# A decoder block on one core: two tiles of the next quarter's first MLP product are computed ahead of a quarter's first weight pair, and the pairs' accumulators are read ahead of the next weights' parts

## The chip, the core and the metric

The kernel runs on one core of a Trainium2 chip. The core has five engines with a queue each: TensorE (PE, matrix products; PEld is its weight load), VectorE (DVE), ScalarE (ACT), GpSimd (POOL) and SyncE (SP, which here only issues transfers). An engine works through its own queue in order, and waits where an operand or a buffer is not ready. The metric is the device time of one execution in microseconds (us), the median over runs.

## The reference

One decoder block for 512 tokens of width 1024. Two token mixers run side by side (a compressed, selected and windowed attention, and a latent attention), are merged by gates and added to x. Then comes the MLP, which the change is about:

```
h2 = modulate(rmsnorm(x1), shift, scale)          # 512 x 1024
u  = square(relu(h2 @ w_fc1))                     # w_fc1: 1024 x 4096
x2 = x1 + gate * (u @ w_fc2)                      # w_fc2: 4096 x 1024
out = rmsnorm(x2, g_final)
```

## The kernel before, in words

**Numbers.** Every float32 operand of a product is split in two parts, hi (rounded for the fast matmul) and lo (the rest), and a product is three matmuls: hi by hi, hi by lo, lo by hi. The hi part is a copy on ACT, the lo part a subtraction on DVE.

**MLP.** The 4096 inner columns are worked through in four quarters of 1024 (the loop over qq). A quarter has two stages.

*Units.* Eight tiles of the first product, in the order UNITS = 0, 4, 1, 5, 2, 6, 3, 7. One tile (`dense`, L197 to L199) has 8 blocks of 128 rows by three matmuls of 512 columns, 24 matmuls, into one accumulator of PSUM (tags acc, acc, m, o in turn). Its weights (`wsplit`, L183 hi and L184 lo) come as one transfer of 512 KB. After each tile `unit_parts` runs: relu on ACT out of the accumulator (L913), and then, for units 0 to 3, two squares (L922, L923), a difference (L924) and the parts uh and ul (L925 ACT, L926 DVE); for units 4 to 7 a square (L933), the parts uh and ul (L934, L935), and the sums and differences t3, t2 and t4 with units 0 to 3 (L942 to L944) and their parts (L946, L947, L949, L950). Unit 7 is the last, so its parts are the last that the pairs need. They all lie in 20 buffers of 512 columns (tag N) and 4 of 1024 (tag kk), and all of these are in use when a quarter's units are done.

*Pairs.* The second product of a quarter adds to x. Two column tiles of w_fc2 by two halves of the rows and two halves of the tokens are computed with seven products in place of eight (sums of weight blocks and of u's blocks, in the manner of Strassen and Winograd). One such pair has seven `product` calls of 12 matmuls of 256 columns (L854), 84 in all, into four accumulators: pa and pb (tag s, two buffers) and pc and pd (tag t, two buffers). A quarter has four pairs; the last quarter has two, and its last four column tiles are computed in the plain way by halves of the tokens, as the tail.

*Weights of a pair* (`pair_weights`, L815): two transfers of 512 KB on SP's queue, four sums on POOL (L825), and the parts (`split_part`, hi L812 on ACT, lo L813 on DVE): one part of 1024 columns for a11 and a12, four of 512 columns for the sums s1 to s4 (ws_hi, ws_lo), one of 512 columns for a22. The buffers decide how early they can be made: the sums' parts take 4 of 5 buffers of tag p per pair (hi and lo of s1 with s3, hi and lo of s2 with s4), so the next pair's are made as the present pair's products let go of them.

*Order within a pair* (`pair_tiles`). Two orders exist. In the usual one the products come as pa (a11), pb (s1), pc (s3), pd (s2), then pa again (a12), pb again (s4), pc again (a22). Between them the accumulators are read, because pa, pb and pc are added onto again: u is a copy of pa (L864), e is a copy of pc (L878) to which pb is added (L879), u gets pd (L881). pb's second product (s4) may only start once L879 has read pb. The first pair of each quarter is "fresh": its order is pa, pb, then a12, s3 and s4 by blocks of rows (units 4 to 6 first, unit 7's block last), then pd and a22, so that what unit 7 makes is wanted late; there e is a copy of pb (L867) to which pc is added (L873), and u gets pd (L875). The two accumulators of tag t go to the next pair as they are read: pc and pd of the next pair wait for L875 and L900. In the second pair of a quarter the scheduler has put pc ahead of pb on PE; in the third and fourth the usual order stands. At the end `sink` reads the accumulators into x: L894 out of pa, L896 on POOL, L898 out of pb, L900 out of pc. The next pair's pb is the same buffer of tag s as this pair's pb, and so waits for L898.

**What sets the order.** The program is written in a plain order, and a scheduler places each instruction in its engine's queue by priority; work under `tc.high_priority()` goes ahead of what is ready beside it. The weights' hi and lo parts (L183, L184, L812, L813) and the relu (L913) are under high priority; of the reads of accumulators only L873 is.

## Time and profile before

| | |
|---|---|
| median of three runs | 853.72 us (852.92 to 855.2) |
| the profiled execution's own time | 852.93 us |
| span from the first to the last instruction in it | 851.2 us |
| mean granted TensorE clock | 0.983 |
| busy: PE, DVE, ACT, POOL | 805.5, 611.8, 393.0, 151.2 us |
| pairs of quarter 1 (520.48 to 570.59) | 50.11 us |
| pairs of quarter 2 (614.15 to 658.89) | 44.74 us |
| pairs of quarter 3 (702.45 to 747.16) | 44.71 us |
| pairs of quarter 4 (790.72 to 816.57, two pairs) | 25.85 us |

1.73 us of the execution lie outside the span. A stage of pairs is counted from the end of the last unit's matmuls to the end of the last pair's. In a row of the timeline, the first number is the start in us from the span's start, the second the duration; in brackets stands the time for which the engine stood idle ahead of it, with what ended that. In a row of the windows view stand the window, its length, and for each engine the busy time with the number of instructions, then the granted clock, the share of busy DMA engines and the GB/s. The waits view gives the total, the times and the longest of each kind.

### The profile page before, as it was taken

What the parts mean: (1) busy time and instruction counts of PE and PEld (TensorE: products, weight loads), DVE (VectorE), ACT (ScalarE), POOL (GpSimd) and SP (SyncE); (2) the same over time, 40 slices, a digit from 0 to 9 for tenths busy, and PEclk for the clock granted to TensorE, in tenths of its full rate; (3) what the DMA queues carried; (4) which work ended last, traced back from release to release, by engine and by line L of the source; (5) the groups of instructions that cost most, each with busy time, mean ns of one, the idle gap of its engine ahead of it and who ended that gap; (6) DMA issues with size and microseconds to landing.
All of it is one profiled execution on the core that took longest, in us unless ns stands there. A gap on an engine that the chain in (4) does not pass through costs nothing.

```text
span 851.2 us, 11895 instructions
## 1 busy us (share of the span) xinstructions
PE 805.5 (95%) x4444; PEld 650.0 (76%) x4444; DVE 611.8 (72%) x1177; ACT 393.0 (46%) x742; POOL 151.2 (18%) x125
## 2 busy tenths in 40 slices
PE   6899999999999999999989998899989998999996
PEld 3687668665586657887769996898789887988895
DVE  6969569878658874568785859775777577756754
ACT  4458436555226442222323457335643565355651
POOL 2400000000001000003300023612352154414200
PEclk8999999999999999999999998999999999999998
DMA  9773342100132214587564212232223322322202
GB/s 340 254 252 112 126 148 66 34 26 26 49 126 73 74 38 161 174 273 225 174 220 172 75 50 75 98 103 97 88 74 115 122 75 75 124 100 84 90 1 99
DMA packets 31004, 99.76 MB, mean 117 GB/s; under 512 B 3521, under 2 KB 5761, under 8 KB 30946
## 3 DMA queue, kind: packets, MB, share of 16 engines
q1 hardware_dynamic: 30880, 98.89, 34.6%
q8 instruction: 35, 0.57, 0.3%
q0 software_dynamic: 64, 0.11, 0.1%
q14 instruction: 23, 0.19, 0.1%
q10 hardware_dynamic: 2, 0.00, 0.0%
HBM read 96.89 MB, written 2.10 MB: 116 GB/s over the span
## 4 chain that ended last, share of the span: by engine, by line
PE 61%; DVE 15%; DMA 7%; issue 6%; ACT 5%; POOL 5%; SPq 0%; POOLq 0%; DVEq 0%; ACTq 0%
PE ps_acc L197 8%; PE ps_acc L198 8%; PE ps_acc L199 8%; PE ps_s L854 7%; PE ps_t L854 4%; DMA w_raw<-in_w_ada_dram 4%; PE ps_t L391 3%; PE ps_o L568 3%; DVE junk L107 3%; POOL wsum L825 3%; DMA w_raw<-in_w_fc_dram 3%; PE ps_s L640 2%; DVE ws_lo L813 2%; DVE w_lo L184 2%; PE ps_o L653 2%
## 5 line engine op out<-in xcount | busy, mean ns | idle before, releaser
L183 ACT ACTIVATE w_hi<-w_raw 128x1024 fp32r<-128x1024 f32 x76 | 80.3, 1058 | 134.9 <-PE ps_acc L198 86.5
L184 DVE TENSOR_TENSOR w_lo<-w_raw,w_hi 128x1024 fp32r<-128x1024 f32 x76 | 96.5, 1271 | 60.9 <-ACT w_hi L183 60.6
L346 ACT ACTIVATE p<-p,nm 128x128 f32<-128x128 f32 (+3 forms) x96 | 53.3, 556 | 58.1 <-DVE nm L344 56.8
L198 PE MATMUL ps_acc<-hl,w_hi 128*128 128x512 f32 x200 | 80.1, 401 | 0.0
L199 PE MATMUL ps_acc<-hh,w_lo 128*128 128x512 f32 x200 | 80.0, 400 | 0.0
L197 PE MATMUL ps_acc<-hh,w_hi 128*128 128x512 f32 x200 | 79.3, 397 | 0.0
L812 ACT ACTIVATE ws_hi<-wsum 128x512 fp32r<-128x512 f32 x56 | 35.2, 631 | 65.6 <-POOL wsum L825 55.7
L379 DVE COPY pT<-ps_t 128x512 f32<-128x512 f32 (+1 forms) x72 | 42.4, 598 | 31.0 <-PE ps_o L568 16.5
L825 POOL TENSOR_TENSOR wsum<-w_raw 128x512 f32<-128x512 f32 x28 | 40.4, 1442 | 102.1 <-DMA w_raw<-in_w_fc_dram 94.1
L825 POOL TENSOR_TENSOR wsum<-wsum,w_raw 128x512 f32<-128x512 f32 x28 | 47.5, 1697 | 35.7 <-DVE ws_lo L813 35.4
L107 DVE SCALAR_TENSOR_TENSOR junk<-w_raw,cb 128x1024 bf16<-128x1024 f32 x32 | 40.0, 1255 | 18.6 <-DMA w_raw<-in_w_ada_dram 18.6
L813 DVE TENSOR_TENSOR ws_lo<-wsum,ws_hi 128x512 fp32r<-128x512 f32 x56 | 46.8, 867 | 7.2 <-PE ps_acc L198 6.3
L198 PEld LDWEIGHTS ps_acc<-hl,w_hi 128*128 128x128 f32 x200 | 37.6, 188 | 10.9 <-issue 4.3
L854 PE MATMUL ps_t<-t,ws_hi 128*128 128x256 f32 x224 | 41.2, 282 | 4.9 <-DVE ue L875 4.9
L199 PEld LDWEIGHTS ps_acc<-hh,w_lo 128*128 128x128 f32 x200 | 37.6, 188 | 10.0 <-issue 3.1
L197 PEld LDWEIGHTS ps_acc<-hh,w_hi 128*128 128x128 f32 x200 | 37.6, 188 | 9.9 <-issue 3.0
L197 PE MATMUL ps_acc<-h2h,w_hi 128*128 128x512 f32 x112 | 43.6, 390 | 0.0
L199 PE MATMUL ps_acc<-h2h,w_lo 128*128 128x512 f32 x112 | 43.6, 389 | 0.0
L198 PE MATMUL ps_acc<-h2l,w_hi 128*128 128x512 f32 x112 | 43.6, 389 | 0.0
L758 POOL TENSOR_TENSOR yb<-ya,yb 128x512 f32<-128x512 f32 x8 | 17.5, 2184 | 135.1 <-DVE yb L757 125.0
L854 PE MATMUL ps_s<-uh,w_hi 128*128 128x256 f32 x112 | 33.1, 296 | 7.9 <-ACT uh L925 6.8
L391 PEld LDWEIGHTS ps_t<-ident,p 128*128 128x128 f32 x240 | 27.7, 141 | 16.4 <-issue 6.3
(471 smaller groups left out, 2313.7 us busy)
## 6 DMA issues: line engine op xcount, KB each, us to landing
w_raw<-in_w_fc_dram SPq DMA_DIRECT2D x64, 512.0 KB, 3.3
w_raw<-in_w_ada_dram SPq DMA_DIRECT2D x32, 512.0 KB, 4.3
w_raw<-in_w_z_dram SPq DMA_DIRECT2D x25, 512.0 KB, 3.5
w_ada<-in_w_ada_dram SPq DMA_DIRECT2D x16, 512.0 KB, 6.1
w_raw<-in_w_c_dram SPq DMA_DIRECT2D x8, 512.0 KB, 4.4
w_raw<-in_w_o_dram SPq DMA_DIRECT2D x8, 512.0 KB, 4.4
w_raw<-in_w_out_dram SPq DMA_DIRECT2D x8, 512.0 KB, 3.4
w_raw<-in_w_g_dram SPq DMA_DIRECT2D x8, 448.0 KB, 6.9
```

Of the source, the lines that this page charges most:

```text
L107: nc.vector.scalar_tensor_tensor(junk, w, 1.0, cb, op0=ALU.mult, op1=ALU.mult, accum_out=mod[:, col:col + 1])
L183: nc.scalar.activation(hi[:, :n], raw[:, :n], AF.Copy)
L184: nc.vector.tensor_tensor(lo[:, :n], raw[:, :n], f(hi[:, :n]), op=ALU.subtract)
L197: nc.tensor.matmul(out, w[0], x[0], start=first, stop=False)
L198: nc.tensor.matmul(out, w[0], x[1], start=False, stop=False)
L199: nc.tensor.matmul(out, w[1], x[0], start=False, stop=last)
L346: nc.scalar.activation(o, o, AF.Exp, bias=nm, scale=-1.0, accum_out=sm)
L379: nc.vector.tensor_copy(dst, src)
L391: nc.tensor.transpose(pp[:, off:off + P], aps[i][:, kb * P:(kb + 1) * P], ident)
L813: nc.vector.tensor_tensor(lo, src, f(hi), op=ALU.subtract)
L825: nc.gpsimd.tensor_tensor(t, sums[x_] if isinstance(x_, int) else x_, y_, op=ALU.add)
L854: nc.tensor.matmul(out, w[a_][:, k], x[k][b_], start=(first and k == 0 and j == 0), stop=(k == 3 and j == 2), skip_group_check=True)
```

## The change

**Two tiles ahead of the first pair.** After a quarter's last unit, in the first three quarters, the first two tiles of the next quarter's first product (units 0 and 4) are computed and their relu is taken, before the quarter's first pair. Their relus need a place to stay (`held0`, `held1`): the first takes a buffer of tag qst; for the second, four small tiles of an earlier stage (w2, th, hd, rep) are put together into two buffers of a new tag "common", one of which is free by then. What follows the relu for these two units (the squares, parts and sums) is written at its place in the next quarter's loop; the relu is taken out of `unit_parts` into `unit_relu`.

**One order for the pairs.** The fresh order goes; every pair has the usual one.

**Reads ahead of parts.** In `pair_tiles` the copies of pa and pc, the additions of pb and pd, and the whole sink stand under high priority.

```diff
-    w2 = sb.tile([P, 2, 2, 64], F32, name="w2")
+    def common(name):
+        return sb.tile([P, S], F32, name=name, tag="common", bufs=2)
+
+    w2_th, hd_rep = common("w2_th"), common("hd_rep")
+    w2 = w2_th[:, 0:256].rearrange("p (k n c) -> p k n c", k=2, n=2)
...
-        th = sb.tile([P, 256], F32, name="th", tag="th")
+        th = w2_th[:, 256:512]
...
-    def pair_tiles(w, b, sink, fresh):
+    def pair_tiles(w, b, sink):
...
         product(pa, w["a11"], b["11"], True)
-        nc.scalar.activation(u, pa, AF.Copy)
+        with tc.high_priority():
+            nc.scalar.activation(u, pa, AF.Copy)
         product(pb, w["s1"], b["t1"], True)
-        if fresh:
-            nc.scalar.activation(e, pb, AF.Copy)
-            for ks in (range(3), range(3, 4)):
-                product(pa, w["a12"], b["21"], False, ks)
-                product(pc, w["s3"], b["t3"], True, ks)
-                product(pb, w["s4"], b["22"], False, ks)
-            with tc.high_priority():
-                nc.vector.tensor_tensor(e, e, pc, op=ALU.add)
-            product(pd, w["s2"], b["t2"], True)
-            nc.vector.tensor_tensor(u, u, pd, op=ALU.add)
-        else:
-            product(pc, w["s3"], b["t3"], True)
+        product(pc, w["s3"], b["t3"], True)
+        with tc.high_priority():
             nc.scalar.activation(e, pc, AF.Copy)
             nc.vector.tensor_tensor(e, e, pb, op=ALU.add)
-            product(pd, w["s2"], b["t2"], True)
+        product(pd, w["s2"], b["t2"], True)
+        with tc.high_priority():
             nc.vector.tensor_tensor(u, u, pd, op=ALU.add)
-            product(pa, w["a12"], b["21"], False)
-            product(pb, w["s4"], b["22"], False)
+        product(pa, w["a12"], b["21"], False)
+        product(pb, w["s4"], b["22"], False)
         product(pc, w["a22"], b["t4"], False)
-        sink(pa, pb, pc, u, e)
+        with tc.high_priority():
+            sink(pa, pb, pc, u, e)
...
-        pair_tiles(w, ub, sink, n == 0)
+        pair_tiles(w, ub, sink)
...
+    held = {}
     for qq in range(4):
...
         for i, n in enumerate(UNITS):
+            if i in held:
+                unit_parts(n, held[i], ub, keep, qq == 3)
+                continue
...
-            unit_parts(n, pa, ub, keep, qq == 3)
+            unit_parts(n, unit_relu(pa, tmp("relu")), ub, keep, qq == 3)
+
+        held = {}
+        if qq < 3:
+            for i in range(2):
+                w = wsplit(d["w_fc1"][8 * qq + 8 + UNITS[i]], (KT, P))
+                pa = psum("acc")
+                dense(pa, w, h2)
+                r = sb.tile([P, S], F32, name=f"held{i}", tag="qst", bufs=NB["qst"]) if i == 0 else common("held1")
+                held[i] = unit_relu(pa, r)
         nf = KT - NH2 if qq == 3 else KT
         for n in range(0, nf, 2):
             fc2_pair(qq, n)
```

The lines move by a few: the sums of weights L825 become L829, the parts L812 and L813 become L816 and L817, the products L854 become L858, the copies L864 and L878 become L869 and L873, the additions L879 and L881 become L874 and L877, the sink's L894, L898 and L900 become L891, L895 and L897, and the relu L913 becomes L908.

Three places show how the queues change. The first is ACT's queue at the end of the second quarter's units, before: the relu of unit 7 (`relu<-ps_o`), its square, its uh, and the parts t of t3 and t24, with the first pair's reads of pa (`ue<-ps_s`, L864 and L867) among them.

```order
L812 ACTIVATE w_hi<-w_raw 128x1024
L913 ACTIVATE relu<-ps_o 128x512
L933 ACTIVATE relu<-relu 128x512
L864 ACTIVATE ue<-ps_s 128x256
L934 ACTIVATE uh_5458<-relu 128x512
L946 ACTIVATE t_5466<-b_5119 128x256
L949 ACTIVATE t_5469<-ur_5419 128x512
L867 ACTIVATE ue<-ps_s 128x256
L812 ACTIVATE w_hi<-w_raw 128x512
```

The same place of the changed kernel; `held` is the kept relu of the next quarter's units 0 and 4.

```order
L908 ACTIVATE relu<-ps_o 128x512
L816 ACTIVATE ws_hi<-wsum 128x512
L932 ACTIVATE relu<-relu 128x512
L933 ACTIVATE uh_5453<-relu 128x512
L945 ACTIVATE t_5461<-b_5180 128x256
L948 ACTIVATE t_5464<-ur_5414 128x512
L816 ACTIVATE w_hi<-w_raw 128x512
L908 ACTIVATE held_5498<-ps_acc 128x512
L921 ACTIVATE b_6065<-held_5498 128x256
L922 ACTIVATE ur_6068<-held_5498 128x256
L816 ACTIVATE w_hi<-w_raw 128x1024
L908 ACTIVATE held_5531<-ps_acc 128x512
```

Unit 7's parts now stand ahead of every read of the first pair's accumulators, and the two held relus with the first squares of the next quarter stand between them and the first pair.

The second is DVE's queue in the first pair of the second quarter, before; xr is a tile of x, v a temporary of the sink.

```order
L894 SCALAR_TENSOR_TENSOR xr_3166<-ps_s,modb,xr_3166 128x256
L873 TENSOR_TENSOR ue<-ue,ps_t 128x256
L813 TENSOR_TENSOR ws_lo<-wsum,ws_hi 128x512 x2
L813 TENSOR_TENSOR w_lo<-w_raw,w_hi 128x512
L813 TENSOR_TENSOR ws_lo<-wsum,ws_hi 128x512 x2
L875 TENSOR_TENSOR ue<-ue,ps_t 128x256
L900 TENSOR_TENSOR v_5598<-ue,ps_t 128x256
L813 TENSOR_TENSOR w_lo<-w_raw,w_hi 128x1024
L898 TENSOR_TENSOR v_5600<-ue,ps_s 128x256
```

And of the changed kernel.

```order
L817 TENSOR_TENSOR w_lo<-w_raw,w_hi 128x1024
L817 TENSOR_TENSOR ws_lo<-wsum,ws_hi 128x512 x2
L874 TENSOR_TENSOR ue<-ue,ps_s 128x256
L877 TENSOR_TENSOR ue<-ue,ps_t 128x256
L891 SCALAR_TENSOR_TENSOR xr_3161<-ps_s,modb,xr_3161 128x256
L817 TENSOR_TENSOR w_lo<-w_raw,w_hi 128x512
L817 TENSOR_TENSOR ws_lo<-wsum,ws_hi 128x512 x2
L895 TENSOR_TENSOR v_5661<-ue,ps_s 128x256
L897 TENSOR_TENSOR v_5659<-ue,ps_t 128x256
```

The read of pd (L875), which stood behind five parts, is gone; what stands in this pair now is what stood in the other pairs before, with the next pair's parts of 1024 and of two sums ahead of the read of pb (L874) and three parts ahead of the read of pb at the end (L895).

The third is DVE's queue in the last pair of the second quarter of the changed kernel, where the held units' parts are made; the first row belongs to the next quarter's unit weights.

```order
L184 TENSOR_TENSOR w_lo<-w_raw,w_hi 128x1024
L925 TENSOR_TENSOR ul_6067<-ur_6068,uh_6066 128x512
L934 TENSOR_TENSOR ul_6075<-held_5531,uh_6074 128x512
L942 SCALAR_TENSOR_TENSOR ur_6068<-ur_6068,held_5531 128x256
L946 TENSOR_TENSOR t_6082<-b_6065,t_6082 128x256
L943 SCALAR_TENSOR_TENSOR ur_6068<-ur_6068,held_5531 128x256
L874 TENSOR_TENSOR ue<-ue,ps_s 128x256
L877 TENSOR_TENSOR ue<-ue,ps_t 128x256
```

Five operations of the held units stand ahead of the last pair's read of pb; before, only the row of L184 stood there. On PE every pair of the changed kernel has the order pa, pb, pc, pd, a12, s4, a22.

More of the change, by code (lines that the diff above doesn't have):

```diff
@@ L443, in hidden @@
             nc.tensor.transpose(pt[:, n * P:(n + 1) * P], th[:, n * P:(n + 1) * P], ident)
-        hd = sb.tile([P, 2, 2, 2, 32], F32, name="hd", tag="hd")
-        nc.vector.tensor_copy(hd.rearrange("p n k g b -> p (n k g b)"), pt[:, 0:256])
+        hd = hd_rep[:, 0:256].rearrange("p (n k g b) -> p n k g b", n=2, k=2, g=2)
+        nc.vector.tensor_copy(hd_rep[:, 0:256], pt[:, 0:256])
         pk = psum("m")
@@ L458, in hidden @@
             for n in range(2):
-                rep = sb.tile([P, 4, 32], F32, name="rep", tag="rep", bufs=2)
+                rep = hd_rep[:, 256 + 128 * n:384 + 128 * n].rearrange("p (r b) -> p r b", r=4)
                 nc.gpsimd.tensor_copy(rep, hd[:, n, 1, g, :][:, None, :].to_broadcast([P, 4, 32]))
@@ L907, in fc2_pair, with unit_relu, unit_parts @@
                 nc.scalar.activation(xt[j], xt[j], AF.Copy, scale=cols[:, C_GFIN + j:C_GFIN + j + 1])
-    def unit_parts(n, pa, ub, keep, last):
-        r = tmp("relu")
+    def unit_relu(pa, r):
         with tc.high_priority():
             nc.scalar.activation(r, pa, AF.Relu)
+        return r
+    def unit_parts(n, r, ub, keep, last):
         hh = big_n(f"uh{n}", F32R)
```

## The prediction

> **What bounds the kernel now.** The page's busy line comes first.
>
> ```profile
> span 851.2 us, 11895 instructions
> PE 805.5 (95%) x4444; PEld 650.0 (76%) x4444; DVE 611.8 (72%) x1177; ACT 393.0 (46%) x742; POOL 151.2 (18%) x125
> ```
>
> PE is the bound: 95% busy. The change adds and removes no matmul, so it can only save time in which PE stands idle or runs slowly. The page's mean does not say where that is; the windows view does. Its first four rows are the pair stages of the four quarters; the fifth is the last pair of quarter 2, in which PE waits for nothing.
>
> ```profile
> 520.48:570.59 50.11, 43.70 (x337) 42.19 (x336) 38.30 (x63) 22.40 (x41) 19.00 (x15) 0.93 0.29 95
> 614.15:658.89 44.74, 40.92 (x337) 39.91 (x336) 34.66 (x55) 19.66 (x35) 18.32 (x14) 1.00 0.28 95
> 702.45:747.16 44.71, 40.92 (x337) 39.91 (x336) 34.69 (x55) 19.63 (x35) 18.31 (x14) 1.00 0.28 95
> 790.72:816.57 25.85, 22.64 (x170) 21.63 (x169) 20.14 (x34) 15.38 (x29) 4.04 (x4) 0.93 0.17 62
> 648.95:658.89 9.94, 9.94 (x86) 9.94 (x85) 6.63 (x13) 2.89 (x4) 0.74 (x1) 1.00 0.36 121
> ```
>
> A pair without waits takes 9.94 us, so 84 matmuls at 0.118 us. Four take 39.76, two take 19.88. What the stages have above that is all the change can reach: 50.11 - 39.76 = 10.35 in quarter 1, 4.98 in quarter 2, 4.95 in quarter 3, 25.85 - 19.88 = 5.97 in quarter 4, together 26.25 us. The waits view of PE from 519 us on names what ends the idle time (total us, times, longest):
>
> ```profile
> PE ps_s L854 <- ACT uh L925: 6.8, 5, 2.7
> PE ps_t L854 <- DVE ue L875: 4.9, 4, 1.5
> PE ps_s L854 <- DVE v L898: 2.9, 7, 0.6
> PE ps_s L854 <- ACT ue L864: 1.1, 1, 1.1
> ```
>
> Four causes: a quarter's first pair finds unit 3's parts uh and ul unfinished; the second pair's pc waits until the first pair's pd is read (L875); a pair's pb waits until the last pair's is read (L898); in quarter 4 PE waits once for the copy L864. PE's timeline gives the places. In quarters 1 and 2:
>
> ```profile
> 522.13 0.39 PE L854 MATMUL ps_s<-uh,w_hi 128*128 128x256 f32 x1 [0.79 <-ACT uh L925]
> 526.10 0.58 PE L854 MATMUL ps_s<-uh,w_hi 128*128 128x256 f32 x1 [2.70 <-ACT uh L925]
> 616.46 0.38 PE L854 MATMUL ps_s<-uh,w_hi 128*128 128x256 f32 x1 [1.08 <-ACT uh L925]
> 617.19 0.39 PE L854 MATMUL ps_s<-ul,w_hi 128*128 128x256 f32 x1 [0.34 <-DVE ul L926]
> 629.13 0.51 PE L854 MATMUL ps_t<-t,ws_hi 128*128 128x256 f32 x2 [1.51 <-DVE ue L875]
> 631.36 0.38 PE L854 MATMUL ps_s<-uh,ws_hi 128*128 128x256 f32 x1 [0.58 <-DVE v L898]
> ...
> 640.42 0.38 PE L854 MATMUL ps_s<-uh,ws_hi 128*128 128x256 f32 x1 [0.31 <-DVE v L898]
> ...
> 650.38 0.28 PE L854 MATMUL ps_s<-uh,ws_hi 128*128 128x256 f32 x1
> ```
>
> A wait costs more than its idle time: matmuls start 0.118 apart, but a row lasts 0.28 (the last one), so the row ahead of a wait counts 0.16 as busy that is lost, and the first one behind it is up to 0.10 longer. I take 0.23 together, an estimate. And two entries cost clock:
>
> ```profile
> 527.00:531.00 4.00, 4.00 (x19) 4.00 (x20) 3.94 (x6) 3.22 (x7) 0.97 (x1) 0.50 0.01 4
> 793.80:797.80 4.00, 4.00 (x21) 4.00 (x22) 3.74 (x7) 3.69 (x8) 0.97 (x1) 0.58 0.03 12
> ```
>
> After 0.79 and 2.70 of idle time quarter 1's entry ran at half the clock: 19 matmuls in 4 us, where 34 fit.
>
> [...]
>
> **The change, part by part.** *Two tiles ahead of the first pair.* They are moved, not added; their 48 matmuls are the same. What they bring is cover: ACT's copies of unit weights stand one tile apart,
>
> ```profile
> 576.04 1.06 ACT L183 ACTIVATE w_hi<-w_raw 128x1024 fp32r<-128x1024 f32 x1 [4.31 <-PE ps_acc L198]
> 581.48 1.06 ACT L183 ACTIVATE w_hi<-w_raw 128x1024 fp32r<-128x1024 f32 x1 [2.02 <-PE ps_acc L198]
> ```
>
> so a tile is 5.44 us and two are 10.88. Against it stands the time that the last units' parts need after the last unit's matmuls. Unit 3's, for which pa waited, took until 526.10 - 520.48 = 5.6 us; the last of all, unit 7's, until 530.33 + 0.68 - 520.48 = 10.5 us in quarter 1, the worst:
>
> ```profile
> 530.33 0.68 DVE L950 TENSOR_TENSOR t<-ur,t 128x512 fp32r<-128x512 f32 x1
> ```
>
> That is in time for the pair's start, and unit 7's t3 and t24 are only wanted by pc and pd, 2.84 and 4.26 us later (24 and 36 matmuls). So the entries' waits and quarter 1's lost clock go. In ACT's queue the held relus and squares stand behind unit 7's parts and ahead of the reads of pa; the last of them needs matmuls that end as the pair begins, and pa must be read by the 48th matmul, 5.68 us later: hidden by those. The two transfers of 512 KB go on SP's queue ahead of the pairs' instead of behind them; the pairs' stages use 0.28 of the DMA engines, so I cost that at nothing. Without that cover it would be a transfer's landing in three places, 3.3 us each by the page's row:
>
> ```profile
> w_raw<-in_w_fc_dram SPq DMA_DIRECT2D x64, 512.0 KB, 3.3
> ```
>
> *The fresh order goes.* With it L875 goes, which came behind five parts for the next pair, the last of them slow:
>
> ```profile
> 626.36 2.38 DVE L813 TENSOR_TENSOR ws_lo<-wsum,ws_hi 128x512 fp32r<-128x512 f32 x2
> 628.67 0.41 DVE L875 TENSOR_TENSOR ue<-ue,ps_t 128x256 f32<-128x256 f32 x1
> ```
>
> The first pair becomes what the others are. What such a pair asks of DVE I read in pair 2 of quarter 2, after which PE does not wait (650.38 above):
>
> ```profile
> 644.23 1.28 DVE L813 TENSOR_TENSOR ws_lo<-wsum,ws_hi 128x512 fp32r<-128x512 f32 x2
> 645.43 0.41 DVE L879 TENSOR_TENSOR ue<-ue,ps_s 128x256 f32<-128x256 f32 x1
> 647.88 0.69 DVE L813 TENSOR_TENSOR w_lo<-w_raw,w_hi 128x512 fp32r<-128x512 f32 x1 [1.08 <-ACT w_hi L812]
> 648.49 1.29 DVE L813 TENSOR_TENSOR ws_lo<-wsum,ws_hi 128x512 fp32r<-128x512 f32 x2
> 649.69 0.41 DVE L898 TENSOR_TENSOR v<-ue,ps_s 128x256 f32<-128x256 f32 x1
> ```
>
> Let T be a pair's start without waits; its pb starts at T + 1.42, so here T = 640.42 - 1.42 = 639.00. The first two sums' parts for the next pair need a buffer that s3 lets go of after 36 matmuls, T + 4.26; here they began at T + 5.23. The read of pb (L879) ended at 645.84, T + 6.84; s4, which waits for it, comes after 60 matmuls, T + 7.10. The last read (L898) ended at 650.10, T + 11.10; the next pb wants it after 96 matmuls, T + 11.36. Both were in time by 0.26 us, in a pair that began its parts 0.97 later than the buffers allow. So a pair of this order has from 0.26 to 1.2 us to spare, and I forecast mostly no wait.
>
> *Reads ahead of parts.* The queues show that DVE still has the next pair's parts ahead of the read of pb (L874) and three ahead of the last one (L895), as in pair 2; what priority gains is that no more work slips between. The waits on L898 are 2.9 us in seven places. From both sides, what stays of them in a quarter is nothing, or 0.58 and 0.31 with 0.23 each, 1.35. I keep 0.58, nearer to pair 2's row without a wait than to the other end. In the last pair of a quarter five operations of the held units stand ahead of the read of pb: two ul at 0.69 and three at 0.42, 2.6 us. They need buffers that pb's operands let go of at T + 2.84, and an ACT copy first, of this kind:
>
> ```profile
> 795.45 0.63 ACT L934 ACTIVATE uh<-relu 128x512 fp32r<-128x512 f32 x1
> ```
>
> So 2.84 + 0.63 + 2.64 + 0.41: the read ends at T + 6.5, 0.6 before s4. The last pair makes no sums' parts that would stand there too. If that cover goes, it costs what it is late.
>
> *Quarter 4.* Nothing is held here, so its entry stays, with these rows:
>
> ```profile
> 793.07 0.39 PE L854 MATMUL ps_s<-uh,w_hi 128*128 128x256 f32 x1 [1.13 <-ACT uh L925]
> 793.80 0.39 PE L854 MATMUL ps_s<-ul,w_hi 128*128 128x256 f32 x1 [0.34 <-DVE ul L926]
> 806.08 0.50 PE L854 MATMUL ps_t<-t,ws_hi 128*128 128x256 f32 x2 [0.40 <-DVE ue L875]
> 806.94 0.39 PE L854 MATMUL ps_s<-uh,ws_hi 128*128 128x256 f32 x1 [0.24 <-DVE v L898]
> 812.20 0.39 PE L854 MATMUL ps_s<-uh,w_hi 128*128 128x256 f32 x1 [1.10 <-ACT ue L864]
> ```
>
> The three lower rows go: 0.40 + 0.24 + 1.10 and about 0.23 behind each, 2.4 us. (The last waits for a copy, which now has priority on ACT.) The two upper rows stay, 1.47 + 0.46 = 1.93, and the rest of the 5.97, 1.6, is the lost clock. New here: the usual order wants unit 7's t3 after 33 matmuls, not 51. Its lo part is this row:
>
> ```profile
> 797.27 0.41 DVE L947 TENSOR_TENSOR t<-t,t 128x256 fp32r<-128x256 f32 x1
> ```
>
> It ends at 797.68; with the clock kept PE would want it at 790.72 + 1.93 + 33 x 0.118 = 796.5, so a wait of 1.1 and 3.3 left with its 0.23. With the clock lost as now, PE comes to it 1.6 later and hardly waits: 3.5 left. Should both come, 4.9. I take 3.3.
>
> **The sum.** Quarter 1: 10.35 - 0.58 = 9.77. Quarter 2: 4.98 - 0.58 = 4.40. Quarter 3: 4.95 - 0.58 = 4.37. Quarter 4: 5.97 - 3.3 = 2.67. Together 21.2 us. The profiled execution took 852.93 with a span of 851.2; 851.2 - 21.2 = 830.0 of span, 831.7 of time. The median of the runs, 853.72, is 0.79 above the profiled one: **832.5 us**. The lower bound is all 26.25 gone: 827.5.
>
> **Rivals.** *Waits of the usual order come back (0.17).* The entries' gain stays, but s4 or the next pb waits in more pairs, since L875's 1.51 and L898's 0.58 and 0.31 had DVE's load as their cause, and that load is the same; 0.26 us is little to spare. Three waits of 2.40 together, as quarter 2 has now, with 0.23 each are 3.09 a quarter in place of 0.58: +7.5 for three quarters, 840.0. Against it: pair 2 left no wait though its parts began late.
>
> *DVE's parts are stretched (0.05).* Here are the two ends of one part's duration, alone and beside POOL's sums (ns, least, median, most):
>
> ```profile
> L813 DVE TENSOR_TENSOR ws_lo<-wsum,ws_hi x56: 677/686/1781, 497.8 to 805.0; 128x512 fp32r<-128x512 f32 x56
> ```
>
> Were both parts ahead of the read of pb stretched in each pair, it would end at 4.26 + 2 x 1.78 + 0.41 = 8.23 against 7.10: 1.13 idle and 0.23, in ten pairs (three in each of quarters 1 to 3, one in quarter 4) 13.6 us: 846.1. Against it: the median is near the least.
>
> [...]
>
> *Slower (0.04).* The next pair's parts (L817) stand ahead of the read of pb (L874) in nine pairs of quarters 1 to 3 and one of quarter 4. If they make s4 wait for about 1.5 us, PE may lose its clock there, as in quarter 4's entry after 1.47 of idle time. That entry cost 1.93 + 1.6 = 3.53; ten such places are 35.3 against the gain of 21.2: 832.5 + 35.3 = 867.8. It decides from 2.1 us a place on, so where L874 ends later than T + 8.6 and the clock goes. Against it: quarter 2 had 1.51 of idle time at L875 and kept clock 1.00.
>
> *No net change (0.04).* The held tiles' cover fails: unit 7's parts run as late as before, because the held relus and the pairs' parts go ahead of them by priority. Then the entries cost as now, and what L875 cost is won and spent again on s4: within 2.6 us of 853.7. Against it: ACT's order has unit 7's parts ahead of the held relus.
>
> **How the numbers follow.** Forecast 0.70, the rivals 0.17, 0.05, 0.04 and 0.04. Of the forecast's own range the lower end is 828 (all waits gone), the upper 837.5 (in three quarters 0.77 more, the other end for L898, and nothing won in quarter 4, 2.67); with the first rival the range is 828 to 842, and 0.8 of the chance lies in it. 0.3%, 2.6 us, is about what a measurement of this kernel can tell from no change. Faster by more: the forecast and the two first rivals, 0.92. Within: 0.04. Slower: 0.04.
>
> **What would show it.** Right: no wait of PE for uh or ul (L924, L925) in the pairs of quarters 1 to 3; clock 1.00 in quarter 1's pairs; pair stages of about 40.3 us in quarters 1 to 3, and 23.2 in quarter 4; no wait named for L874 above 0.3 us. Wrong: PE waits for L874 or for L895 in several pairs of a quarter (first or second rival, told apart by the duration of the parts ahead); a clock under 0.95 in quarters 2 or 3 (third); waits for uh at the pairs' start (fourth). A span above 842 would say that the order of the pairs costs more than I read from pair 2.

## The result, and the profile after

The changed kernel takes **831.36 us** in the median (828.15 to 832.16), the kernel before 853.44 in the same comparison (852.92 to 855.2): a ratio of 0.973, with a 95% interval from 0.970 to 0.976. The forecast was 832.5, with a range from 828 to 842. The profiled execution has a span of 829.8 us, 21.4 less than before; 830.0 was forecast.

The page of the changed kernel, its first lines:

```profile
span 829.8 us, 11895 instructions
PE 798.3 (96%) x4444; PEld 646.3 (78%) x4444; DVE 606.2 (73%) x1177; ACT 392.1 (47%) x742; POOL 148.0 (18%) x125
```

The windows view, the pair stages of the four quarters (columns as in the prediction):

```profile
530.21:572.12 41.91, 40.59 (x338) 39.77 (x336) 36.01 (x58) 20.92 (x38) 18.48 (x16) 1.00 0.35 114
615.67:655.37 39.70, 39.70 (x337) 39.69 (x336) 32.78 (x54) 19.36 (x35) 16.85 (x14) 1.00 0.33 107
698.93:738.71 39.78, 39.78 (x337) 39.78 (x336) 32.66 (x53) 19.35 (x35) 16.74 (x14) 1.00 0.33 107
771.39:794.92 23.53, 20.87 (x170) 20.07 (x169) 19.52 (x35) 16.27 (x30) 4.03 (x4) 1.00 0.22 68
```

In quarters 2 and 3 PE is busy for the whole stage: four pairs in 39.70 and 39.78 us, where four pairs without a wait were reckoned at 39.76. The clock is 1.00 in all four stages. What the stages have above 39.76 (and 19.88 for the two pairs of quarter 4) fell from 26.25 us to 2.15 - 0.06 + 0.02 + 3.65 = 5.76. That is 20.5 of the 21.4 us of span. The rest lies outside these stages: the first pair started at 530.21, of which 10.88 are the two moved tiles, so 1.15 earlier than before, and what follows the last pair took 0.25 longer. In the profiles below that start, less the tiles moved ahead of it, lies anywhere between 516.4 and 520.9, and between 516.7 and 519.3 in the change's own two profiles; so I compare stages and give the ratio of the times beside them.

The waits view of PE from 510 us on shows what is left:

```profile
PE ps_s L858 <- ACT uh L924: 1.6, 1, 1.6
...
PE ps_s L858 <- DVE v L895: 0.6, 2, 0.4
PE ps_s L858 <- ACT ue L869: 0.5, 1, 0.5
PE ps_t L858 <- DVE t L946: 0.4, 1, 0.4
PE ps_s L858 <- DVE ul L925: 0.3, 1, 0.3
PE ps_t L858 <- ACT t L945: 0.3, 1, 0.3
...
PE ps_s L858 <- DVE ue L874: 0.2, 1, 0.2
```

The waits for uh, ul and t are those of quarter 4's entry; the others lie in quarter 1. The wait on the read of pd, 4.9 us before, is gone.

### The profile page after: what moved, and what is told of

Read it like the earlier page. It is cut to its first block, busy times and chain, and to the rows that moved or that the text cites. A ratio compares the mean times of both kernels' runs of the same rounds, so it can differ in the third digit from the quotient of the medians.

```text
span 829.8 us, 11895 instructions
## 1 busy us (share of the span) xinstructions
PE 798.3 (96%) x4444; PEld 646.3 (78%) x4444; DVE 606.2 (73%) x1177; ACT 392.1 (47%) x742; POOL 148.0 (18%) x125
## 4 chain that ended last, share of the span: by engine, by line
PE 74%; DVE 11%; DMA 5%; ACT 3%; POOL 3%; issue 3%; SPq 0%; DVEq 0%; POOLq 0%; ACTq 0%
PE ps_acc L197 10%; PE ps_acc L199 10%; PE ps_acc L198 10%; PE ps_s L858 8%; PE ps_t L858 6%; PE ps_t L391 4%; DVE junk L107 3%; PE ps_o L572 3%; DMA w_raw<-in_w_ada_dram 3%; PE ps_s L644 2%; PE ps_o L657 2%; PE ps_s L197 1%; PE ps_s L198 1%; PE ps_s L199 1%; POOL yb L762 1%
## 5 line engine op out<-in xcount | busy, mean ns | idle before, releaser
L184 DVE TENSOR_TENSOR w_lo<-w_raw,w_hi 128x1024 fp32r<-128x1024 f32 x76 | 96.1, 1266 | 62.8 <-ACT w_hi L183 62.4
L816 ACT ACTIVATE ws_hi<-wsum 128x512 fp32r<-128x512 f32 x56 | 35.3, 631 | 58.0 <-POOL wsum L829 55.3
L829 POOL TENSOR_TENSOR wsum<-w_raw 128x512 f32<-128x512 f32 x28 | 39.5, 1410 | 64.9 <-DMA w_raw<-in_w_fc_dram 53.4
L829 POOL TENSOR_TENSOR wsum<-wsum,w_raw 128x512 f32<-128x512 f32 x28 | 45.9, 1640 | 25.6 <-DVE ws_lo L817 25.2
L817 DVE TENSOR_TENSOR ws_lo<-wsum,ws_hi 128x512 fp32r<-128x512 f32 x56 | 42.9, 796 | 4.9 <-ACT ws_hi L816 2.5
L858 PE MATMUL ps_t<-t,ws_hi 128*128 128x256 f32 x224 | 40.5, 281 | 0.7 <-DVE t L946 0.4
L817 DVE TENSOR_TENSOR w_lo<-w_raw,w_hi 128x1024 fp32r<-128x1024 f32 (+1 forms) x28 | 31.0, 1107 | 10.2 <-ACT w_hi L816 10.2
```

Of the source, the lines that this page charges most:

```text
L184: nc.vector.tensor_tensor(lo[:, :n], raw[:, :n], f(hi[:, :n]), op=ALU.subtract)
L817: nc.vector.tensor_tensor(lo, src, f(hi), op=ALU.subtract)
L829: nc.gpsimd.tensor_tensor(t, sums[x_] if isinstance(x_, int) else x_, y_, op=ALU.add)
L858: nc.tensor.matmul(out, w[a_][:, k], x[k][b_], start=(first and k == 0 and j == 0), stop=(k == 3 and j == 2), skip_group_check=True)
```

## The experiments

All stages in us, from the windows view of each run's profile; "above" is the sum of what the four stages have above pairs without waits.

| run | median | ratio to before (95%) | Q1 | Q2 | Q3 | Q4 | above |
|---|---|---|---|---|---|---|---|
| before | 853.44 | | 50.11 | 44.74 | 44.71 | 25.85 | 26.25 |
| the change | 831.36 | 0.973 (0.970 to 0.976) | 41.91 | 39.70 | 39.78 | 23.53 | 5.76 |
| the change again | 830.39 | 0.973 (0.971 to 0.976) | 41.58 | 39.70 | 39.78 | 23.17 | 5.07 |
| held tiles alone | 847.23 | 0.993 (0.991 to 0.995) | 49.21 | 43.68 | 43.50 | 26.41 | 23.64 |
| held tiles, squares behind | 843.60 | 0.991 (0.988 to 0.994) | 46.53 | 42.78 | 42.79 | 25.68 | 18.62 |
| held tiles, own order, priority | 846.31 | 0.993 (0.990 to 0.995) | 48.87 | 44.04 | 43.89 | 24.33 | 21.97 |
| one order with priority, nothing held | 841.31 | 0.986 (0.984 to 0.989) | 47.25 | 42.30 | 42.39 | 23.17 | 15.95 |
| the change without priority | 829.67 | 0.973 (0.971 to 0.976) | 41.25 | 39.71 | 39.80 | 23.61 | 5.21 |
| one held tile | 833.02 | 0.977 (0.974 to 0.980) | 44.83 | 39.78 | 39.70 | 23.51 | 8.66 |
| two more on DVE per pair | 847.15 | 0.995 (0.993 to 0.997) | 47.13 | 44.84 | 44.84 | 24.88 | 22.53 |
| second pair's parts and more behind | 832.26 | 0.976 (0.974 to 0.978) | 42.09 | 40.43 | 39.85 | 23.11 | 6.32 |
| the same without the third group | 833.02 | 0.978 (0.975 to 0.980) | 42.33 | 40.44 | 40.07 | 23.65 | 7.33 |
| rearranged in quarter 4 alone | 828.11 | 0.972 (0.970 to 0.974) | 41.57 | 39.79 | 39.69 | 21.60 | 3.49 |

Four more operations on DVE per pair: 878.27, 1.031 (1.026 to 1.035); there some matmuls of the next units stand between the last pair's, so its stages are not comparable.

Each stage comes from one profile. The medians fall by 0.6 to 3.2 us more than the stages do, and of all fourteen profiles the one before has the second latest start of the MLP; so of a difference between runs I take from the stages what it is made of, and its size only roughly.

### The held tiles alone

```diff
-        pair_tiles(w, ub, sink)
+        pair_tiles(w, ub, sink, n == 0)     # pair_tiles as in the kernel before
```

> The two held tiles alone; the first pair of each quarter keeps its own order and no read of an accumulator has priority beyond what it had before. My theory (the stages' excess is two separate things: the entries, 7.2 us in quarter 1 and 1.9 in each of quarters 2 and 3, and the first pairs' waits on L875 and L898, 3.1 in each): the entries' 11.0 us go, the 3.1 stay: about 842.4, with waits of PE on the addition of pd (1.5 each) still in the trace and none on uh or ul in quarters 1 to 3. Rival (the order and the priorities bring nearly all, the tiles only move the wait): 850 or more. Rival (the tiles alone do it): 833 or less.

847.23, between my 842.4 and the first rival's 850: 2.6 us less in the stages, not 11.0 (3.2 in quarters 1 to 3, and quarter 4, where nothing is held, took 0.6 more). The windows view of the first two stages and of 4 us in the first, ACT's timeline there, and PE's:

```profile
528.59:577.80 49.21, 43.07 (x337) 42.26 (x336) 36.21 (x58) 21.12 (x38) 19.38 (x16) 0.93 0.29 97
621.36:665.04 43.68, 40.72 (x337) 39.92 (x336) 33.33 (x54) 19.54 (x35) 18.12 (x14) 1.00 0.28 98
535.00:539.00 4.00, 3.99 (x18) 4.00 (x19) 0.00 (x0) 0.23 (x1) 0.54 (x1) 0.50 0.02 8
```
```profile
531.87 0.42 ACT L928 ACTIVATE b<-held 128x256 f32<-128x256 f32 x1
...
534.05 0.63 ACT L939 ACTIVATE held<-held 128x512 f32<-128x512 f32 x1
534.59 0.36 ACT L868 ACTIVATE ue<-ps_s 128x256 f32<-128x256 f32 x1
```
```profile
535.01 0.58 PE L858 MATMUL ps_s<-uh,w_hi 128*128 128x256 f32 x1 [3.41 <-ACT ue L868]
```

The waits on uh and ul are gone, and a new one has come in their place: pa's second product, which the first pair's own order wants after 24 matmuls, waits 3.41 us for the copy of pa. That copy stands on ACT behind unit 7's parts, both held relus and the held units' squares, up to 534.59. The clock falls to 0.50 behind it, as it did at the entry before. The read of pd still costs its 1.5 to 1.9 in each of quarters 1 to 3.

### The held units' squares behind the first pair's copies

```diff
+                with tc.issue_after(first.ins):      # the first pair's copy of pb
-                unit_parts(n, held[i], ub, keep, qq == 3)
+                    unit_parts(n, held[i], ub, keep, qq == 3)
```

> The held tiles with the first pair's own order, as in the run of the held tiles alone (847.23), but the held units' squares (two of 256 columns and one of 512 on ACT) are queued behind the first pair's copies of pa and pb. PE's and POOL's queues are the same. In the run of the held tiles alone pa's second product, which this order wants after 24 matmuls, waited 3.41, 0.54 and 0.45 us for the copy of pa, which stood on ACT behind unit 7's parts and these squares. My theory (the held tiles' own work on ACT took up the place of the wait they removed; the usual order hides it since it wants pa's second product only after 48 matmuls): the three squares are 0.9 to 1.3 us on ACT, so the two waits of 0.5 go and quarter 1's falls to some 2.1: 2 to 4 us less, 843 to 845. Rival (unit 7's parts alone hold the copy up): no change, 847.

843.6, and PE's timeline has:

```profile
533.26 0.38 PE L858 MATMUL ps_s<-uh,w_hi 128*128 128x256 f32 x1 [1.99 <-ACT ue L868]
```

3.41 became 1.99, the waits of 0.5 in quarters 2 and 3 went, 5.0 us in the stages (0.7 of them in quarter 4, which the edit does not touch), 3.6 in the median. So the held tiles' own work on ACT was part of the new wait; unit 7's parts, the held relus and two parts of weights still stand ahead of the copy.

### Held tiles, the first pair's own order, and priority for the reads

```diff
         if fresh:
...
-            nc.vector.tensor_tensor(u, u, pd, op=ALU.add)
+            with tc.high_priority():
+                nc.vector.tensor_tensor(u, u, pd, op=ALU.add)     # and so for the other reads
```

> Held tiles, and all reads of accumulators under high priority, but the first pair of each quarter keeps its own order. In DVE's queue the read of pd now stands ahead of the last two of the five parts that it stood behind. My theory (L875 was late for its place behind parts, not for the order itself): most of 1.7 us goes in each of quarters 1 to 3 and 0.6 in quarter 4: 836 to 838. Rival (the order itself costs the wait): as with the held tiles alone, 842.

846.31, no better than the held tiles alone, as the rival has it. In PE's timeline of quarter 2 the wait on the read of pd is gone, and these have come:

```profile
636.31 0.39 PE L858 MATMUL ps_s<-uh,ws_hi 128*128 128x256 f32 x1 [2.04 <-DVE v L909]
...
640.05 0.48 PE L858 MATMUL ps_t<-t,ws_hi 128*128 128x256 f32 x2 [0.73 <-DVE v L911]
```

L909 and L911 are the sink's reads of pb and pc. The parts that the read of pd overtook now stand in front of these. In this order pb and pc are finished late and the next pair wants their buffers early; which read stands first only chooses where PE waits.

### One order with priority, and nothing held

```diff
-        if qq < 3:
+        if False:
```

> One order for all pairs and the priorities, without the held tiles. My theory: 2.8 us a quarter are won in the pairs and 2.3 in quarter 4, but at the entries, which stay, the usual order wants unit 7's t3 earlier and waits some 1.2 us for it in each quarter: 846, with waits on uh, ul and t3 at every entry, and a lost clock in quarter 1. Rival (the order needs the tiles' cover and costs more than it brings without it): 853 or more. Rival (order and tiles add up without a new wait): 842.

841.31, better than the 846 of my theory and close to its last rival. PE's waits view has, beside 1.4 for ul, these two:

```profile
PE ps_s L858 <- ACT uh L924: 6.6, 5, 2.7
...
PE ps_t L858 <- DVE t L946: 1.2, 3, 0.4
```

Within the pairs nothing is left: not a wait on L874 or L895. 10.3 us go in the stages, of them 2.3 to 2.9 in each quarter. The new wait on t3 that I had put at 1.2 a quarter is there, but only 0.4 at a time: PE comes late to it, since uh has held it up before.

The two single parts bring 2.6 and 10.3 us in the stages, together 12.9. The change brings 20.5 to 21.2. Some 8 us are their working together. By the medians the two bring 5.8 and 11.8 and the change 22.1, so 4.5 us together, with some 2 us of uncertainty on each of the three: that the parts need each other is shown, how much it is worth is known only roughly.

### The change without the priority

```diff
-        with tc.high_priority():
-            sink(pa, pb, pc, u, e)
+        sink(pa, pb, pc, u, e)               # and so for the four reads above it
```

> The change without the priorities on the reads. The queues of PE, DVE and POOL are then the same as the change's, row for row; on ACT eleven rows stand elsewhere (a hi part ahead of the copies of pa and pc in place of behind them). My theory: nothing depends on these, 831.4 within 1.5. Rival (the reads' priority is what keeps s4 from waiting): PE waits for the addition of pb in several pairs, 836 or more.

829.67, the ratio of the change to the last digit that counts. The waits of PE in its pairs:

```profile
PE ps_s L858 <- ACT uh L920: 1.4, 1, 1.4
...
PE ps_s L858 <- DVE v L891: 0.6, 2, 0.4
...
PE ps_s L858 <- DVE ue L872: 0.2, 1, 0.2
```

The second thing that the change is named after, reads ahead of the weights' parts, moves eleven rows on ACT and none elsewhere, and does nothing that can be measured.

### One held tile

```diff
-            for i in range(2):
+            for i in range(1):
```

> The change with one held tile in place of two, so 5.44 us of cover in place of 10.88. My theory (cover has to reach to the last part of unit 7 that pc wants, not only to unit 3's parts): waits for t3 come, some 3 us in quarter 1 and 1 in each of quarters 2 and 3: 834 to 837. Rival (unit 3's parts were all that was late, 2 to 5.6 us): within 1 of the change. Rival (it is worth half): 841.

833.02, 2.9 us more than the change in the stages, all of it in quarter 1. The windows view of stages 1 and 2, and PE's timeline in stage 1:

```profile
523.20:568.03 44.83, 42.17 (x337) 41.35 (x336) 36.92 (x61) 21.64 (x39) 16.98 (x14) 0.96 0.32 106
611.59:651.37 39.78, 39.78 (x337) 39.75 (x336) 32.95 (x53) 18.18 (x33) 16.66 (x14) 1.00 0.33 107
```
```profile
526.24 0.39 PE L858 MATMUL ps_s<-uh,w_hi 128*128 128x256 f32 x1 [1.78 <-ACT uh L924]
```

One tile is enough in quarters 2 and 3. The second earns its place in quarter 1 alone, and not by t3, as I had it: unit 3's uh is late there even with 5.44 us of cover.

### Two and four more operations on DVE in each pair

```diff
             nc.scalar.activation(e, pc, AF.Copy)
+            for _ in range(2):               # 4 in the other run
+                nc.vector.tensor_tensor(e, e, e, op=ALU.max)
             nc.vector.tensor_tensor(e, e, pb, op=ALU.add)
```

The lines that hold PE's matmuls to the change's order are left out here.

> The change with two more operations on VectorE in each pair ahead of the read of pb: the larger of e and e, which leaves e as it is, 256 columns each, so 0.66 to 0.8 us later. PE's queue is held to the same order. In the trace of the change the read of pb ends 1.13, 0.75, 0.27 and 0.9 us before s4 in the four pairs of quarter 2. My theory (what counts is the time to spare at s4, and VectorE's idle time behind it makes good the rest): only the third pair waits, 0.4 with 0.2 for the refill: 1 to 3 us more in all. Rival (VectorE is the bound in the pairs, any work added to it shows): 14 pairs at 0.7, 10 us more. Rival (there is no time to spare, each pair waits): 14 pairs at 0.7 + 0.23, 13 more.

> The same with four operations, 1.33 to 1.6 us later. My theory (time to spare of 0.3 to 1.1 at s4): waits of 0.2 to 1.1 with 0.2 for the refill in nearly every pair, some 3.4 a quarter, 8 to 13 us more than the change. Rival (VectorE as the bound): 20 more. Rival (more time to spare than read): under 3 more.

847.15 and 878.27, 16 and 47 us more than the change: far above my theory's 1 to 3 and 8 to 13, and above the rivals too. First the size of the added operation with two of them (ns: least, median, most), then DVE's and POOL's timelines and PE's in the first pair of quarter 2:

```profile
L877 DVE TENSOR_TENSOR ue<-ue x28: 410/1158/1512, 537.0 to 806.8; 128x256 f32<-128x256 f32 x28
```
```profile
625.41 1.51 DVE L877 TENSOR_TENSOR ue<-ue 128x256 f32<-128x256 f32 x1
626.85 0.41 DVE L881 TENSOR_TENSOR ue<-ue,ps_t 128x256 f32<-128x256 f32 x1
627.18 1.16 DVE L877 TENSOR_TENSOR ue<-ue 128x256 f32<-128x256 f32 x1
```
```profile
624.97 1.67 POOL L829 TENSOR_TENSOR wsum<-wsum,w_raw 128x512 f32<-128x512 f32 x1 [1.06 <-DVE ws_lo L817]
626.60 1.45 POOL L829 TENSOR_TENSOR wsum<-w_raw 128x512 f32<-128x512 f32 x1
```
```profile
628.85 0.38 PE L860 MATMUL ps_s<-uh,ws_hi 128*128 128x256 f32 x1 [1.72 <-DVE ue L878]
```

The dose was larger than written: 0.41 us alone, 1.51 and 1.16 beside POOL's sums, and the scheduler put the read of pd (0.33 from its start to the next) between. So the read of pb came 1.51 + 0.33 + 1.16, about 3 us later, against the 1.13 to spare that I had read: some 1.8 should be left as a wait, and 1.72 is there. The other pairs of that quarter agree: counted from the pair's start the read ended 2.96, 2.57, 1.44 and 0.20 us later than in the change, with 1.13, 0.75, 0.27 and 0.9 to spare, and PE waited 1.72, 1.71, 0.97 and nothing. The mechanism stands, the time to spare was read rightly, and the added time was not. PE waits for nothing else in the pairs of quarters 2 and 3, so the rival that any work on DVE shows fails: of 3 us only the part above the time to spare does.

With four, the read of pb is 2.8 to 5.0 us late in ten pairs, and the clock falls. The waits view, and the windows behind two of these waits, one of 4.97 us and one of 3.50:

```profile
PE ps_s L860 <- DVE ue L878: 33.5, 10, 5.0
```
```profile
544.50:548.50 4.00, 3.66 (x18) 3.66 (x19) 1.29 (x3) 0.63 (x1) 0.81 (x2) 0.57 0.40 131
659.00:663.00 4.00, 3.73 (x32) 3.73 (x33) 2.31 (x6) 0.63 (x1) 1.91 (x2) 1.00 0.34 131
```

This is the slower rival's mechanism, brought about by force: 26 us more than before. Its condition, a wait of about 1.5 us, was put too short: with two operations, five waits of 1.7 us and one of 3.17 lost no clock; with four, eight of ten waits from 2.76 to 4.97 did, and those ending at 659 and 672 did not. The last section says what tells them apart.

### Looking for what is left: three rearrangements

The first puts the second pair's parts, the tail's four copies and the held units' parts behind chosen instructions on ACT and DVE; the second leaves out the third group. The change ran beside them once more.

```diff
+        with behind(ends):          # ends: unit 7's last parts on ACT and DVE, for the second pair
-        split_part(raw[0], hi, lo)
+            split_part(raw[0], hi, lo)
...
+        with behind(keep["end"]):
-        nc.scalar.activation(hi, b12, AF.Copy)
+            nc.scalar.activation(hi, b12, AF.Copy)
...
+                with behind(first):
-                unit_parts(n, held[i], ub, keep, qq == 3)
+                    unit_parts(n, held[i], ub, keep, qq == 3)
```

> The change itself once more, beside the two kernels after it. 0.973 of the kernel before, about 831; pair stages as in its first profile (41.9, 39.7, 39.8, 23.5 us) within 0.7, while the start of the first pair may differ by up to 3 us from 530.2, as it did among the runs so far, for reasons that lie ahead of the MLP.

> The change, with three groups of work queued behind a chosen instruction on ACT and DVE: the parts of a quarter's second pair and the four copies for the tail (L995, L996 in the change) behind unit 7's last parts, and the held units' parts behind the first pair's copy of pc and read of pb. In the change's trace quarter 4's ACT stood idle for 2.02 us in front of a hi part of the second pair, with unit 6's square and unit 3's relu queued behind it; unit 3's uh came 1.65 us late and unit 7's t3 0.67. My theory (quarter 4's 3.65 us and quarter 1's 2.15 come from this place in the queues): quarter 4's stage falls from 23.5 to 20.5 to 21.5, quarter 1's from 41.9 to 40.3 to 41.3: 2.5 to 4.5 us less than the change. Rival (the second pair's parts, made later, are late for that pair): waits on them or on the reads of pb there, no gain. Rival (the entry of quarter 4 is bound by unit 3's own chain of five operations): under 1 us less.

> The same without the third group: the held units' parts stay where the change has them. My theory: quarter 4 as in the run before this one, quarter 1 between 40.8 and 41.9, since the held units' squares still stand ahead of the first pair's copies there. Rival (nothing differs): the two runs agree within 0.3 us in quarter 1.

No gain: 832.26 and 833.02 against 830.39, and in quarter 4 ACT's idle time had only moved. ACT's and POOL's timelines of the first of them:

```profile
771.57 0.42 ACT L950 ACTIVATE t<-t 128x256 fp32r<-128x256 f32 x1 [3.67 <-POOL t L946]
...
772.93 0.58 ACT L913 ACTIVATE relu<-ps_m 128x512 f32<-128x512 f32 x1
```
```profile
767.67 1.29 POOL L829 TENSOR_TENSOR wsum<-w_raw 128x512 f32<-128x512 f32 x1 [7.40 <-DMA w_raw<-in_w_fc_dram]
768.92 1.47 POOL L829 TENSOR_TENSOR wsum<-wsum,w_raw 128x512 f32<-128x512 f32 x1
770.35 1.19 POOL L946 TENSOR_TENSOR t<-relu,b 128x256 f32<-128x256 f32 x1
```

Unit 6's t3 stands on POOL behind two sums whose weights land at 767.67; ACT, which works in order, stands at t3's part until 771.57, and unit 3's relu stands behind it. Quarter 1's copy of pa, which the third group was for, no longer waits with it (0.94 without), but the second pair's parts, made later, cost 1.1 there at the next pb.

The last run changes quarter 4 alone, with POOL's sums in it:

```diff
+            with behind(ends[:1]):   # unit 6's t3 on POOL; quarter 4's second pair only
-            nc.gpsimd.tensor_tensor(t, sums[x_] if isinstance(x_, int) else x_, y_, op=ALU.add)
+                nc.gpsimd.tensor_tensor(t, sums[x_] if isinstance(x_, int) else x_, y_, op=ALU.add)
```

> The change, with the rearrangement in quarter 4 alone: the second pair's sums on POOL behind unit 6's t3, its parts on ACT and DVE behind unit 7's last parts, and the tail's four copies behind those too. In the two runs before, ACT's idle time had moved, in quarter 4, from the hi part of the second pair (2.0 us) to unit 6's t3 (3.67 us), which stood on POOL behind two sums whose weights had landed late; unit 3's relu stood behind it on ACT, so unit 3's uh still came 1.4 to 1.7 us late. My theory (that chain - landing, sums, t3, ACT's queue, relu, uh - is the entry's wait): ACT's idle time goes, uh comes in time or under 0.5 late, quarter 4's stage falls from 23.2 to between 20.3 and 21.3, 2 to 3 us less than the change: about 828. Rival (unit 3's own five operations on ACT and DVE after its matmuls are the wait): the stage stays within 0.5 of 23.2. Rival (the second pair's sums come too late for it): waits at that pair, no gain.

```profile
765.03 0.42 ACT L951 ACTIVATE t<-t 128x256 fp32r<-128x256 f32 x1 [0.42 <-POOL t L945]
...
766.40 0.58 ACT L912 ACTIVATE relu<-ps_m 128x512 f32<-128x512 f32 x1
```
```profile
770.42:792.02 21.60, 20.79 (x169) 19.91 (x168) 19.25 (x33) 15.93 (x28) 4.19 (x4) 1.00 0.22 74
```

ACT waits 0.42 in place of 3.67 us, unit 3's relu runs ahead of the pair's start in place of behind it, and the stage, 23.53 and 23.17 us in the change's two profiles, takes 21.60, close to the expected 20.3 to 21.3. PE no longer waits for uh at the entry, only 0.34 us for ul. The chain was the right one. In the whole time, 828.11 with a ratio of 0.972 (0.970 to 0.974), it can't be told from the change's 0.973.

## Why the prediction was right

**The bound and the sum.** Right. The gain was to be found in the pair stages and nowhere else, and there 21.2 us were forecast; 20.5 and 21.2 were measured in the change's two profiles. By quarters, forecast against the two profiles: 9.77 against 8.20 and 8.53; 4.40 against 5.04 twice; 4.37 against 4.93 twice; 2.67 against 2.32 and 2.68. That the total came so close is in part luck: quarter 1 brought 1.2 to 1.6 us less than forecast and quarters 2 and 3 together 1.2 more, for separate reasons. No term of the forecast stands for the 1.15 us by which the MLP began earlier.

**The entries.** Right in what it said: no wait on uh or ul in quarters 1 to 3, clock 1.00. Wrong in one sentence, that the copy of pa is hidden in every quarter. In quarter 1 of the change, DVE's, ACT's and PE's timelines have:

```profile
532.22 0.41 DVE L946 TENSOR_TENSOR t<-b,t 128x256 fp32r<-128x256 f32 x1
...
536.16 0.37 ACT L869 ACTIVATE ue<-ps_s 128x256 f32<-128x256 f32 x1
...
536.58 0.39 PE L858 MATMUL ps_s<-uh,w_hi 128*128 128x256 f32 x1 [0.53 <-ACT ue L869]
```

The 10.5 us that unit 7's parts need, read from the kernel before, did not hold either: t3's lo part ended at 532.63, 13.3 us after the last unit's matmuls (530.21 - 10.88 = 519.33). It was in time only because pc wants it 33 matmuls into the pair, at 534.1. The cover was just enough, not ample, and quarter 1 kept 2.15 us where I had left 0.58: the copy's 0.53, the read of pb 0.22, the next pairs' pb 0.37 and 0.20, and about 0.23 behind each.

**The fresh order goes.** Right, and more so than I dared say: in quarters 2 and 3 no wait was left, where I had kept 0.58 each. The 0.26 us to spare that I read from the third pair before is there unchanged. DVE's read of pb and PE's s4 in that pair of the change:

```profile
641.91 0.41 DVE L874 TENSOR_TENSOR ue<-ue,ps_s 128x256 f32<-128x256 f32 x1
```
```profile
642.59 0.28 PE L858 MATMUL ps_s<-uh,ws_hi 128*128 128x256 f32 x1
```

It ends at 642.32, 0.27 ahead of s4. The run with the added operations showed that this time to spare is what counts. In the last pairs of quarters 1 to 3, where I had reckoned with 0.6 us to spare behind five operations of the held units, it was 0.87 to 1.20.

**The priorities.** I gave them a purpose ("no more work slips between") that the run without them refutes: they have none here.

**Quarter 4.** The term was 3.3 left, by two ways with nearly one price: the clock kept and a wait for t3, or the clock lost and t3 in time. Both occurred. Two windows of 4 us behind the entry, of the change's second profile and of the run without priority:

```profile
772.00:776.00 4.00, 3.34 (x27) 2.94 (x26) 3.81 (x6) 3.09 (x7) 0.97 (x1) 1.00 0.00 0
```
```profile
771.00:775.00 4.00, 3.79 (x19) 3.79 (x20) 3.74 (x7) 3.65 (x7) 0.97 (x1) 0.57 0.11 45
```

The stages took 23.17 and 23.61: left were 3.3 and 3.7. The sizes inside partly cancel: PE waited 1.29 and 1.65 us for uh in the change's two profiles, where I had 1.13, and 0.66 for t3, where I had 1.1. And the entry did not have to stay: the last experiment shows that it hung on the order of work on POOL and ACT.

One reading in the forecast was wrong and changed nothing: the first pair's own order wanted unit 7's t3 after 54 matmuls, not 51.

**What the prediction did not see.** Its sum goes by quarters, with both parts of the change in place; but its account goes part by part, and I took each to bring its share alone. For the tiles alone I wrote down 11.0 us, and that failed. The tiles alone bring 2.6, since with the first pair's own order the copy of pa is wanted 2.84 us sooner and the held tiles' work on ACT stands in front of it. The usual order brings 10.3 alone, and with it the tiles bring the other 10. The sum came out right because it has the copy's turn at the 48th matmul, which only the usual order gives it.

**The rivals.** The waits of the usual order did not come back in quarters 2 and 3; quarter 1 has three of them, 0.8 us together. The stretching of DVE's parts is there in the change too, but it takes from time that is to spare: at 623.68, in quarter 2, a part of 512 columns took 1.28 us beside POOL's operation, against 0.68 at 615.70 beside none, and PE waited for nothing. Only quarter 1 shows some of it: a part that took 1.23 us at 536.89 stands ahead of the read of pb for which PE waited 0.22. The clock was 1.00 in all pair stages of the change, where PE waited 0.22 us at most for L874; it fell in the run with four operations, behind eight of ten waits of 2.76 to 4.97.

In the run with two added operations, the 12 of the 28 that lay beside no sum on POOL took 0.41 to 0.43 us, the 16 beside one 1.16 to 1.51. The read of pd at 626.85, one of whose inputs is an accumulator, took 0.41 beside the sum that began at 626.60.

## What to carry to other kernels

Cover and the order behind it have to be looked at together: work that is moved ahead to hide a wait brings its own instructions on the other engines, and they stand in their queues in front of the very reads that the next stage wants (3.41 us of waiting for the copy of pa, with the held tiles alone). Read the time to spare at each point where the bound engine waits (end of the read against its matmul's start); in these runs added work cost what exceeded it, and nothing up to it. And compare the queues before giving a priority a reason: here no row moved that anyone waited for, and it did nothing.

## What the runs showed of the hardware that I had not expected

The clock's fall at quarter 4's entry is not set by the wait's length. In the change's two profiles it stayed at 1.00 after waits of 1.65 and 1.29 us; without the priorities, with the same queue on PE, it fell to 0.57 after 1.40, and in the kernel before to 0.58 after 1.13. The traces show what the fall goes with. In each of the fourteen, all changes of the granted clock from 400 us on to the last pair lie on one grid of 3.413 us, 70 changes to within 0.002 us. The fall goes with PE's work within one window of that grid. I reckon this work as 0.118 us for a matmul of 256 columns and twice that for one of 512. The MLPs of the fourteen traces have 1229 windows at full clock. Of these, 19 held 1.33 us of work or less, and the clock fell at the end of each; 11 held 1.39 to 1.46, and it fell after two; the rest held more, and it fell after none. At quarter 4's entry the window with the wait held 1.32 us of work in the run without priorities; it held 1.75 and 1.78 in the change's profiles, where it began earlier, among the last unit's matmuls. So in these traces a wait of one length went with a lost clock or with a kept one, by where it lay on the grid. Three windows of the run with four operations show it for two waits of 3.50 us:

```profile
640.55:643.96 3.41, 0.07 (x1) 0.00 (x0) 3.34 (x7) 0.76 (x2) 0.99 (x1) 1.00 0.43 154
654.20:657.62 3.42, 1.57 (x14) 1.36 (x12) 3.35 (x5) 1.15 (x2) 2.49 (x2) 1.00 0.36 110
657.62:661.03 3.41, 1.76 (x15) 1.76 (x16) 1.72 (x5) 0.02 (x1) 0.74 (x1) 1.00 0.38 145
```

The wait that ended at 644.12 fills the first window, and the clock fell at its end. The one that ended at 659.27 lies in the other two, which held 1.39 and 1.70 us of work, and the clock stayed. This is read over the traces; no run was made to test it, and between 1.39 and 1.46 us it does not decide: the kernel before, with 1.41, lies there.

The added VectorE operation of 256 columns, 0.41 us alone, took up to 1.51 beside GpSimd's sums, 3.7 times as long. Two of them per pair so cost 17 us in the stages.
